# Hybrid decoder layer: the output projection in another token order, the down part's first blocks in other memory, the last norm's left sums made in an earlier product

## The chip, the cores and the metric

The kernel runs on one core of a Trainium2 chip, in one launch. A core has TensorE (PE, matmuls, with a separate queue PEld for weight loads), VectorE (DVE), ScalarE (ACT), GpSimd (POOL) and SyncE (SP), which here issues all large transfers. Engines run their own instruction lists in order and wait for one another by semaphores. The metric is device microseconds (us) of one execution; lower is better.

## The reference

One layer for 1024 tokens of width 1024, all in float32, cut to its last part:

```python
def rmsnorm(x, g):
    y = x * lax.rsqrt(jnp.mean(x * x, axis=-1, keepdims=True) + NORM_EPS) * g
...
h = rmsnorm(x, norm_mix)
# h @ w_in feeds a sparse attention (nsa_out) and a retention (ret_out)
mix = sigmoid(gate_a) * (nsa_out @ w_proj_a) + sigmoid(gate_b) * (ret_out @ w_proj_b)
x = x + mix @ w_out
h = rmsnorm(x, norm_mlp)
x = x + jnp.square(jax.nn.relu(h @ w_up)) @ w_down        # hidden width 4096
return rmsnorm(x, norm_final)
```

The change touches everything from `mix @ w_out` on.

## The kernel before, in words

**Number format.** A float32 operand is split into a high and a low part (`h`, `l`; `bh`, `bl`; `wh`, `wl`): ACT copies it to the high part, DVE (or POOL) subtracts that from the original. A product is then three matmuls, high x high, high x low and low x high, added up in a PSUM bank; one is 128x128 by 128x512.

**Output projection** (lines 1144 to 1170). For each half `c` of the output columns and each of the eight token tiles `j` (128 tokens), `dense_tok` makes `mix @ w_out` on PE, and DVE adds the residual (`x1t`, line 1157). In the second half `norm_a` (ACT: sum of squares) and POOL (`rstd`) make the norm, and DVE the normed tile `h` (line 198; named h2 in the code). The normed tile is then transposed by PE into two banks (`put_t`, `tp<-ident,h`, line 1102; there are two such banks) by one of two functions:

- `first_half`, tiles 0 to 3: the transposes are split into `bh` and `bl`.
- `second_half`, tiles 4 to 7: they are combined with the transposes of tile `j-4` into four more forms of the up part's moving operand (sums and differences of the token halves and of the input halves). The tile `j-4` is rebuilt by POOL as `bh + bl` (lines 1122, 1123). The forms go to `bh`/`bl` and to `th`/`tl` (line 1107).

`later` and `tick` put this work `T_LAG` = 4 ticks behind: a tick comes after every second k-block of a product, so the transposes of a tile stand on PE behind the dense product of the tile that comes two later. Those of the last two tiles stand among the first products of the up part (`up_first(0)`, `up_first(1)`).

**Up part.** `h @ w_up` in 16 pairs `p` of hidden blocks. Each pair takes seven products instead of eight (a scheme of sums and differences): forms 11, 21, 2, 3, 1, 4 and 22 of the tokens against as many forms of the weights (`sf` is a sum or difference of weight blocks, lines 1182 to 1185; `wh`, `wl` are split by line 1025/1026). Forms 2, 3 and 4 are read from `th`/`tl`. The results `u11`, `u21`, `u12`, `u22` and the sums `s1`, `s2`, `s4` go to `u_scr` in device memory (line 1221).

**Down part.** Seven products again, `n` = 1, 2, 7, 6, 5, 4, 3, each of 8 groups of 24 matmuls: hidden values from `u_scr` (line 1253, `raw`) against blocks of `w_down` (line 1259; `y11` are the eight blocks of the first product). They are added up in `ac1` to `ac4` on ACT, DVE and POOL; `add_x1` adds the residual on POOL.

**Finish.** `finish` makes the last norm of a token tile: ACT squares and sums both column halves, POOL adds the two sums and makes `rstd` (lines 1302, 188, 189), DVE scales both halves (line 1306), SP stores. Tiles 4 to 7 are finished in the last product, tiles 0 to 3 at the very end: there PE makes the last twelve matmuls of a tile, DVE adds the bank to `ac1` (line 1352), then comes `finish`.

**What sets the order.** Each engine's instructions keep the order that a scheduler gave them at build time from the program text; memory areas (pools) can be reused, and then the first writer of the new area waits for the last reader of the old one. The pool `res` (eight tiles of 128x1024) lies on the right side over areas of the up part.

## Time and profile before

| | us |
|---|---|
| median of 3 runs | 1624.87 |
| lowest, highest | 1623.61, 1625.33 |
| the profiled execution | 1623.7 |
| its span | 1621.9 |
| PE busy in it | 1566.8 |

The span runs from the first to the last instruction of the profiled execution; its own time is 1.8 us more than that. The granted clock of TensorE was 0.986 of full speed on average. The out projection's second half runs from about 916 to 967, the up part from there to 1296, the down part to 1611.

### The profile page before, as it was taken

What the parts mean: (1) busy time and instruction counts of PE and PEld (TensorE: products, weight loads), DVE (VectorE), ACT (ScalarE), POOL (GpSimd) and SP (SyncE); (2) the same over time, 40 slices, a digit from 0 to 9 for tenths busy, and PEclk for the clock granted to TensorE, in tenths of its full rate; (3) what the DMA queues carried; (4) which work ended last, traced back from release to release, by engine and by line L of the source; (5) the groups of instructions that cost most, each with busy time, mean ns of one, the idle gap of its engine ahead of it and who ended that gap; (6) DMA issues with size and microseconds to landing.
All of it is one profiled execution on the core that took longest, in us unless ns stands there. A gap on an engine that the chain in (4) does not pass through costs nothing.

```text
span 1621.9 us, 22739 instructions
## 1 busy us (share of the span) xinstructions
PE 1566.8 (97%) x7876; PEld 1306.9 (81%) x7876; DVE 1037.2 (64%) x2127; ACT 727.1 (45%) x1611; POOL 484.8 (30%) x565
## 2 busy tenths in 40 slices
PE   7999999999999999999999996999999989999997
PEld 5888887987888888888788874888888768888885
DVE  5665663564777777776654268766666548776464
ACT  5454454664766766676421144222222134343352
POOL 5110010001323323333000035665555216523561
PEclk8999999999999999999999997999999999999999
DMA  6101110252111111121644431444444497763472
GB/s 218 65 14 66 56 32 25 83 171 75 44 36 53 47 33 59 47 66 53 201 150 149 156 104 65 152 165 158 157 148 143 145 324 266 233 206 120 140 255 102
DMA packets 99347, 193.93 MB, mean 120 GB/s; under 512 B 26016, under 2 KB 28448, under 8 KB 99232
## 3 DMA queue, kind: packets, MB, share of 16 engines
q1 hardware_dynamic: 99232, 192.48, 35.1%
q8 instruction: 62, 1.02, 0.3%
q14 instruction: 53, 0.43, 0.1%
HBM read 142.11 MB, written 50.33 MB: 119 GB/s over the span
## 4 chain that ended last, share of the span: by engine, by line
PE 84%; POOL 4%; DVE 4%; ACT 4%; issue 2%; DMA 2%; SPq 0%; DVEq 0%; POOLq 0%; ACTq 0%
PE mm L154 23%; PE mmu L154 22%; PE mmd L154 16%; PE gps L154 8%; PE S L154 4%; PE O L154 3%; PE pt L890 2%; PE pt L889 2%; ACT pW L844 1%; DVE S L835 1%; PE pO L154 1%; DVE pl L892 1%; PE pc L154 1%; POOL ac L1312 1%; ACT pS L844 1%
## 5 line engine op out<-in xcount | busy, mean ns | idle before, releaser
L1025 ACT ACTIVATE wh<-raw 128x1024 fp32r<-128x1024 f32 x120 | 123.7, 1056 | 292.7 <-PE mmu L154 141.1
L1026 DVE TENSOR_TENSOR wl<-raw,wh 128x1024 fp32r<-128x1024 f32 x120 | 183.6, 1554 | 89.8 <-ACT wh L1025 89.8
L154 PE MATMUL mmd<-wh 128*128 128x512 f32 x448 | 175.5, 392 | 6.1 <-ACT wh L1025 6.1
L154 PE MATMUL mm<-wh,bh 128*128 128x512 f32 (+1 forms) x448 | 177.0, 395 | 1.5 <-ACT n L578 1.0
L154 PE MATMUL mmd<-wl,wh 128*128 128x512 f32 x448 | 175.4, 392 | 1.0 <-DVE wl L1026 1.0
L154 PE MATMUL mmd<-wh,wl 128*128 128x512 f32 x448 | 175.2, 391 | 0.0
L154 PE MATMUL mm<-wh,bl 128*128 128x512 f32 (+1 forms) x448 | 171.3, 382 | 2.7 <-DVE bl L208 2.7
L154 PE MATMUL mm<-wl,bh 128*128 128x512 f32 (+1 forms) x448 | 171.2, 382 | 0.5 <-DVE wl L182 0.5
L892 DVE TENSOR_TENSOR pl<-pt,ph 128x512 fp32r<-128x512 f32 (+1 forms) x160 | 103.7, 648 | 30.2 <-ACT ph L891 27.7
L188 POOL TENSOR_SCALAR msq<-ssq 128x1 f32<-128x1 f32 (+1 forms) x32 | 7.7, 242 | 372.7 <-ACT h L194 193.0
L891 ACT ACTIVATE ph<-pt 128x512 fp32r<-128x512 f32 (+1 forms) x160 | 90.3, 567 | 55.0 <-PE pt L890 50.4
L854 POOL TENSOR_SCALAR pS<-pS,cf 128x1024 f32<-128x1024 f32 (+7 forms) x64 | 47.8, 748 | 220.3 <-DVE cf L852 69.5
L835 DVE CUSTOM_DVE_ANT_0 S<-S,edge_m 128x512 f32<-128x512 f32 (+3 forms) x192 | 100.6, 530 | 14.9 <-PE S L154 12.9
L154 PE MATMUL gps<-bh,wh 128*128 128x512 f32 x256 | 108.1, 422 | 0.3 <-ACT gst L748 0.2
L154 PEld LDWEIGHTS mmd<-wh 128*128 128x128 f32 x448 | 84.6, 189 | 24.2 <-ACT wh L1025 6.5
L154 PE MATMUL mmu<-bh,wl 128*128 128x512 f32 x256 | 100.4, 392 | 1.5 <-DVE wl L1026 1.5
L154 PEld LDWEIGHTS mm<-wh,bl 128*128 128x128 f32 x448 | 84.7, 189 | 21.2 <-DVE bl L208 3.7
L154 PE MATMUL gps<-bh,wl 128*128 128x512 f32 x256 | 100.9, 394 | 0.0
L154 PE MATMUL gps<-bl,wh 128*128 128x512 f32 x256 | 100.8, 394 | 0.0
L154 PE MATMUL mmu<-bh,wh 128*128 128x512 f32 x256 | 100.6, 393 | 0.0
L154 PE MATMUL mmu<-bl,wh 128*128 128x512 f32 x256 | 100.4, 392 | 0.0
L154 PEld LDWEIGHTS mmd<-wl,wh 128*128 128x128 f32 x448 | 84.7, 189 | 19.5 <-DVE wl L1026 2.0
(294 smaller groups left out, 4051.3 us busy)
## 6 DMA issues: line engine op xcount, KB each, us to landing
raw<-u_scr SPq DMA_DIRECT2D x56, 512.0 KB, 3.9
raw<-w_down SPq DMA_DIRECT2D x40, 512.0 KB, 4.9
raw<-w_up SPq DMA_DIRECT2D x32, 512.0 KB, 3.3
u_scr<-u SPq DMA_DIRECT2D x64, 256.0 KB, 2.0
u_scr<-s SPq DMA_DIRECT2D x48, 256.0 KB, 2.0
y<-w_down SPq DMA_DIRECT2D x16, 512.0 KB, 6.6
x<-x SPq DMA_DIRECT2D x8, 512.0 KB, 3.7
qt<-q_scr SPq DMA_DIRECT2D x32, 128.0 KB, 2.4
```

Source lines behind the costliest of these rows:

```text
L154: T.matmul(o, w, m, start=start, stop=stop)
L188: G.tensor_scalar(m[:, :w], ssq, 1.0 / n, EPS, op0=OP.mult, op1=OP.add)
L835: V.tensor_tensor_reduce(sc, sc, mk, -0.125, BIGPOS, OP.add, OP.min, mx[:, b:b + 1])
L844: A.activation(o, sc, AF.Exp, bias=mx[:, m:m + 1], scale=-1.0, accum_out=sums[:, b:b + 1])
L854: G.tensor_scalar(v, v, cf[:, b:b + 1], 1.0, op0=OP.mult, op1=OP.mult)
L889: T.transpose(tp[:, bi * 2], p0, ident)
L890: T.transpose(tp[:, bi * 2 + 1], p1, ident)
L891: A.activation(ph[:, :n], tp[:, :n], AF.Copy)
L892: V.tensor_sub(pl[:, :n], tp[:, :n], ph[:, :n])
L1025: A.activation(h[:, :n], r, AF.Copy)
L1026: V.tensor_sub(l[:, :n], r, h[:, :n])
L1312: G.tensor_tensor(t, t, x, op=OP.add)
```

## The change

Four things are edited.

1. Tokens go through the out projection in the order 0, 1, 4, 2, 5, 3, 6, 7. `first_half` keeps a plain copy of each bank of transposes (`raw_t`, ACT), and `second_half` uses it in place of the POOL sums `bh + bl`.
2. `th` and `tl` become three pairs of tiles, `t2`, `t3`, `t4`, in the same pool.
3. The eight `y11` blocks get a pool of their own, `res2`, after `acc`; the four banks of the first down product are taken in another order; the first two loads of hidden values are written into the last pair of the up part (`s_load`).
4. `finish`: mean and epsilon are folded into small DVE operations; for tiles 0 to 3 the left half's sum of squares and its multiplication by the norm's gain are made when the product n = 2 is complete and its residual is added (`sums_of`, written in the branch n = 5, placed by the scheduler in the product n = 7), and ACT scales the left half at the end.

The diff, cut to its core:

```diff
@@ -1039,18 +1039,21 @@
-        th_ = formp.tile([P, 12, 512], F32R, name="th")
-        tl_ = formp.tile([P, 12, 512], F32R, name="tl")
+        tf_ = {i: [formp.tile([P, 4, 512], F32R, name=f"t{i}{x}") for x in "hl"] for i in (2, 3, 4)}
...
@@ -1106,32 +1109,33 @@
+            raw_t = {}
+
             def first_half(h, j, q):
                 tp = put_t(h, q)
                 ks = slice(4 * q, 4 * q + 4)
                 split_ps(tp, bh[:, ks, cols(j)], bl[:, ks, cols(j)])
+                raw_t[j, q] = frm.tile([P, 4, P], F32, name=f"raw_t{q}", bufs=2)
+                A.activation(raw_t[j, q], tp, AF.Copy)
 
             def second_half(h, j):
                 i = cols(j - 4)
                 js = cols(j)
+                y11, y21 = raw_t[j - 4, 0], raw_t[j - 4, 1]
...
-                G.tensor_tensor(y11, bh[:, :4, i], bl[:, :4, i], op=OP.add)
-                G.tensor_tensor(y21, bh[:, 4:, i], bl[:, 4:, i], op=OP.add)
                 A.activation(y12, tp, AF.Copy)
-                V.tensor_sub(y11, y12, y11)
+                V.tensor_sub(y11, tp, y11)
...
@@ -1145,14 +1149,14 @@
-                for j in range(NT):
+                for n, j in enumerate((0, 1, 4, 2, 5, 3, 6, 7)):
...
@@ -1220,6 +1224,11 @@
+        def s_load(i, g):
+            r = wraw.tile([P, 1024], F32, name="raw", tag="raw")
+            nc.sync.dma_start(r, flat(u_scr[i][:, 2 * g:2 * g + 2]))
+            return r
@@ -1228,6 +1237,8 @@
+            else:
+                s_raw0 = [s_load(0, 0), s_load(0, 1)]
             up_rest(p, X, s, p < 2)
@@ -1237,21 +1248,17 @@
     res = ctx.enter_context(tc.tile_pool(name="res", bufs=8, side="right", reuse_waits="tile"))
+    acc = ctx.enter_context(tc.tile_pool(name="acc", bufs=4, side="right", reuse_waits="tile"))
+    res2 = ctx.enter_context(tc.tile_pool(name="res2", bufs=8, side="right", reuse_waits="tile"))
     wr7 = ctx.enter_context(tc.tile_pool(name="wr7", bufs=3, reuse_waits="tile"))
     rw2 = ctx.enter_context(tc.tile_pool(name="rw2", bufs=3, reuse_waits="tile"))
-    acc = ctx.enter_context(tc.tile_pool(name="acc", bufs=4, side="right", reuse_waits="tile"))
...
-            t = y11[g] = wd(0, 0, g, res, name="y11")
+            t = y11[g] = wd(0, 0, g, res2, name="y11")
@@ -1293,17 +1300,28 @@
+    def sums_of(t, o):
+        y = tmp.tile([P, 512], F32, name="yq8")
+        A.activation(y, t, AF.Square, accum_out=o)
+
-    def finish(j, c0, c1):
+    def finish(j, c0, c1, pre=None):
         ss = tmp.tile([P, 2], F32, name="ss8")
         y = tmp.tile([P, D], F32, name="y8")
-        for c, t in ((0, c0), (1, c1)):
-            A.activation(y[:, c * 512:(c + 1) * 512], t, AF.Square, accum_out=ss[:, c:c + 1])
-        sq = tmp.tile([P, 1], F32, name="sq8")
-        G.tensor_add(sq, ss[:, 0:1], ss[:, 1:2])
-        r = rstd_of(sq, D, tmp)
+        if pre is None:
+            sums_of(c0, ss[:, 0:1])
+            pre = tmp.tile([P, 1], F32, name="pre8")
+            V.tensor_scalar(pre, ss[:, 0:1], 1.0 / D, EPS, op0=OP.mult, op1=OP.add)
+        sums_of(c1, ss[:, 1:2])
+        m = tmp.tile([P, 1], F32, name="m8")
+        r = tmp.tile([P, 1], F32, name="r8")
+        V.scalar_tensor_tensor(m, ss[:, 1:2], 1.0 / D, pre, op0=OP.mult, op1=OP.add)
+        G.tensor_tensor(r, m, nhalf[:, :1], op=OP.pow)
         for c, t in ((0, c0), (1, c1)):
             cs = slice(c * 512, (c + 1) * 512)
-            V.scalar_tensor_tensor(y[:, cs], t, r, gain3[:, cs], op0=OP.mult, op1=OP.mult)
+            if c == 0 and j < 4:
+                A.activation(y[:, cs], t, AF.Copy, scale=r)
+            else:
+                V.scalar_tensor_tensor(y[:, cs], t, r, gain3[:, cs], op0=OP.mult, op1=OP.mult)
...
+        if step == 0:
+            bank = bank[2:] + bank[:2]
...
             elif n == 5:
                 A.activation(A4[i], b, AF.Copy)
                 G.tensor_tensor(A1[i], A1[i], A4[i], op=OP.add)
+                sums_of(A2[i], pres[i][:, 1:2])
+                V.tensor_scalar(pres[i][:, 0:1], pres[i][:, 1:2], 1.0 / D, EPS, op0=OP.mult, op1=OP.add)
+                G.tensor_tensor(A2[i], A2[i], gain3[:, :512], op=OP.mult)
...
-                finish(i, A2[i], A1[i])
+                finish(i, A2[i], A1[i], pres[i][:, 0:1])
```

How instructions move, at three places. First DVE at the end of the out projection, before: `x1t` of tile 7 is added, `wl` is the low part of the first up weights, and then comes the second half of tile 6 (`y11_10856` and on).

```order
L1107 TENSOR_TENSOR tl_10176<-y21_10789,th_10175 128x4x128
L1157 TENSOR_TENSOR x1t_10823<-mmu_10826,x1t_10823 128x512
L1026 TENSOR_TENSOR wl_10902<-raw_10899,wh_10901 128x1024
L1125 TENSOR_TENSOR y11_10856<-y12_10857,y11_10856 128x512
L198 SCALAR_TENSOR_TENSOR h2_10885<-x1t_10823,rstd_10889,gain_10189 128x1024
L1127 TENSOR_TENSOR f2_10859<-tp_10864,y11_10856 128x512
L1128 TENSOR_TENSOR y12_10857<-tp_10864,y12_10857 128x512
```

The same place of the changed kernel: `bl_84<-tp_10876` and `bl_84<-tp_10916` are the low parts of tile 3, and tile 6's second half begins with `raw_t0_10762`, the kept copy of tile 2.

```order
L1110 TENSOR_TENSOR t4l_10180<-raw_t1_10670,t4h_10179 128x4x128
L1161 TENSOR_TENSOR x1t_10848<-mmu_10851,x1t_10848 128x512
L1110 TENSOR_TENSOR bl_84<-tp_10876,bh_83 128x4x128
L1026 TENSOR_TENSOR wl_10905<-raw_10902,wh_10904 128x1024
L198 SCALAR_TENSOR_TENSOR h2_10888<-x1t_10848,rstd_10892,gain_10193 128x1024
L1110 TENSOR_TENSOR bl_84<-tp_10916,bh_83 128x4x128
L1129 TENSOR_TENSOR raw_t0_10762<-tp_10948,raw_t0_10762 128x512
```

Tile 3's first half has moved behind the last dense product's addition, where before tile 5's second half had just ended; the second halves of tiles 6 and 7 follow in both.

The second place is SP's list at the end of the up part, before: stores of the last pair (`u11_13270` to `s4_13338`), a load of hidden values (`raw_13541`) and the first blocks of `w_down` (`y11_...`).

```order
L1221 DMA u_scr0_76<-u11_13270 128x512
L1221 DMA u_scr5_81<-u22_13300 128x512
L1221 DMA u_scr1_77<-u21_13301 128x512
L1253 DMA raw_13541<-u_scr0_76 128x1024
L1259 DMA y11_13403<-w_down 128x2x512
L1221 DMA u_scr2_78<-u12_13302 128x512
L1221 DMA u_scr3_79<-s2_13337 128x512
L1221 DMA u_scr4_80<-s1_13336 128x512
L1221 DMA u_scr6_82<-s4_13338 128x512
L1259 DMA y11_13439<-w_down 128x2x512
L1259 DMA y11_13475<-w_down 128x2x512
```

The same list of the changed kernel:

```order
L1225 DMA u_scr0_76<-u11_13278 128x512
L1225 DMA u_scr5_81<-u22_13308 128x512
L1266 DMA y11_13416<-w_down 128x2x512
L1225 DMA u_scr1_77<-u21_13309 128x512
L1266 DMA y11_13450<-w_down 128x2x512
L1266 DMA y11_13486<-w_down 128x2x512
L1225 DMA u_scr2_78<-u12_13310 128x512
L1225 DMA u_scr3_79<-s2_13345 128x512
L1225 DMA u_scr4_80<-s1_13344 128x512
L1225 DMA u_scr6_82<-s4_13346 128x512
L1266 DMA y11_13522<-w_down 128x2x512
L1229 DMA raw_13552<-u_scr0_76 128x1024
```

The first `w_down` block stands two places earlier, the next two stand ahead of the stores of `u12` and of the sums, and the load of hidden values stands behind them.

The third place is DVE's end of the program, two of the last four tiles, before:

```order
L1352 TENSOR_TENSOR ac1_13377<-mmd_15317,ac1_13377 128x512
L1306 SCALAR_TENSOR_TENSOR y8_15575<-ac2_13381,rstd_15581,gain_13375 128x512
L1306 SCALAR_TENSOR_TENSOR y8_15575<-ac1_13377,rstd_15581,gain_13375 128x512
L1352 TENSOR_TENSOR ac1_13378<-mmd_15318,ac1_13378 128x512
L1306 SCALAR_TENSOR_TENSOR y8_15602<-ac2_13382,rstd_15608,gain_13375 128x512
L1306 SCALAR_TENSOR_TENSOR y8_15602<-ac1_13378,rstd_15608,gain_13375 128x512
```

and of the changed kernel, where `m8` is 128x1:

```order
L1376 TENSOR_TENSOR ac1_13392<-mmd_15352,ac1_13392 128x512
L1317 SCALAR_TENSOR_TENSOR m8_15613<-ss8_15609,pre_13388 128x1
L1324 SCALAR_TENSOR_TENSOR y8_15610<-ac1_13392,r8_15614,gain_13386 128x512
L1376 TENSOR_TENSOR ac1_13393<-mmd_15353,ac1_13393 128x512
L1317 SCALAR_TENSOR_TENSOR m8_15638<-ss8_15634,pre_13389 128x1
L1324 SCALAR_TENSOR_TENSOR y8_15635<-ac1_13393,r8_15639,gain_13386 128x512
```

One of the two 128x512 scalings has gone to ACT, and a 128x1 operation has come.

## Rows read from the trace of the kernel before

In a row of the timeline the columns are: start in us, length in us, engine, line, operation, output<-inputs, shapes, number of instructions, and in brackets the idle time ahead of it with what ended it.

**Rows 1.** The page: PE's busy time with share and instructions (first row), and PE's busy tenths in 40 equal slices of the span (second row).

```profile
PE 1566.8 (97%) x7876; PEld 1306.9 (81%) x7876; DVE 1037.2 (64%) x2127; ACT 727.1 (45%) x1611; POOL 484.8 (30%) x565
...
PE   7999999999999999999999996999999989999997
```

**Rows 2.** Windows of the span. Columns: window, its length, busy us (and instructions) of PE, PEld, DVE, ACT, POOL, then the granted clock of TensorE, the DMA engines' busy share, GB/s.

```profile
970.00:990.00 20.00, 9.80 (x38) 7.21 (x37) 18.17 (x18) 9.20 (x16) 15.64 (x12) 0.76 0.04 14
990.00:1010.00 20.00, 13.87 (x52) 10.57 (x51) 15.68 (x20) 8.14 (x12) 10.74 (x8) 0.82 0.26 85
...
1290.00:1310.00 20.00, 12.96 (x47) 9.94 (x46) 9.15 (x11) 4.85 (x5) 5.01 (x4) 0.83 0.61 209
...
1610.00:1622.00 12.00, 0.94 (x5) 0.44 (x3) 4.91 (x8) 2.17 (x6) 1.86 (x6) 0.71 0.34 131
```

**Rows 3.** PE's waits from 860 us to the end. Columns: what waits, what for, us in total, times, longest us.

```profile
PE tp L1102 <- DVE bl L1107: 7.5, 2, 4.6
PE mmd L154 <- ACT wh L1025: 6.1, 1, 6.1
```

**Rows 4.** Timeline of PE around the first seam: transposes of tile 5, second matmul of the first up product, second transposes of tile 7, and the first matmul behind the last stop.

```profile
966.56 1.03 PE L1102 MATMUL tp<-ident,h 128*128 128x128 f32 x8
...
967.66 0.40 PE L154 MATMUL mmu<-bl,wh 128*128 128x512 f32 x1
...
985.92 1.09 PE L1102 MATMUL tp<-ident,h 128*128 128x128 f32 x4 [2.93 <-DVE bl L1107]
...
1001.27 0.80 PE L154 MATMUL mmu<-th,wl 128*128 128x512 f32 x1 [4.36 <-DVE wl L1026]
```

**Rows 5.** Timeline of DVE from the last dense products to the first seam: residual additions of three tiles, the first subtraction of a second half, and `sf`.

```profile
947.59 0.69 DVE L1157 TENSOR_TENSOR x1t<-mmu,x1t 128x512 f32<-128x512 f32 x1
...
953.99 0.69 DVE L1157 TENSOR_TENSOR x1t<-mmu,x1t 128x512 f32<-128x512 f32 x1
...
961.45 0.69 DVE L1125 TENSOR_TENSOR y<-y,y 128x512 f32<-128x512 f32 x1 [0.38 <-ACT y L1124]
...
969.65 0.68 DVE L1157 TENSOR_TENSOR x1t<-mmu,x1t 128x512 f32<-128x512 f32 x1
...
991.43 1.78 DVE L1184 TENSOR_TENSOR sf<-raw 128x512 f32<-128x512 f32 x1 [1.18 <-POOL raw L1183]
```

**Rows 6.** Timelines of ACT (a high part from a bank) and of POOL at the first seam.

```profile
941.63 0.60 ACT L1106 ACTIVATE bh<-tp 128x512 fp32r<-128x512 f32 x1 [2.88 <-PE tp L1102]
...
984.59 1.72 POOL L1130 TENSOR_TENSOR y<-y,f 128x512 f32<-128x512 f32 x1
986.27 1.75 POOL L1122 TENSOR_TENSOR y<-bh,bl 128x512 f32<-128x512 f32 x1
...
991.36 1.30 POOL L1123 TENSOR_TENSOR y<-bh,bl 128x512 f32<-128x512 f32 x1
```

**Rows 7.** The second seam: timelines of PE, ACT, DVE and of SP's queue, the DMA issues between 1280 and 1300 us (out<-in, queue, count, KB each, median us from issue to landing), and a window (columns as in rows 2).

```profile
1302.30 0.80 PE L154 MATMUL mmd<-wh 128*128 128x512 f32 x1 [6.09 <-ACT wh L1025]
1304.05 0.80 PE L154 MATMUL mmd<-wl,wh 128*128 128x512 f32 x1 [0.95 <-DVE wl L1026]
...
1301.19 1.06 ACT L1025 ACTIVATE wh<-y 128x1024 fp32r<-128x1024 f32 x1 [6.83 <-DMA y<-w_down]
...
1302.28 1.72 DVE L1026 TENSOR_TENSOR wl<-y,wh 128x1024 fp32r<-128x1024 f32 x1 [4.61 <-ACT wh L1025]
...
1292.78 2.57 SPq L1221 DMA_DIRECT2D u_scr<-u  x2
...
1296.58 0.39 SPq L1259 DMA_DIRECT2D y<-w_down  x1
...
raw<-u_scr SPq DMA_DIRECT2D x1, 512.0 KB, 3.6
y<-w_down SPq DMA_DIRECT2D x1, 512.0 KB, 4.5
...
1304.00:1308.00 4.00, 3.95 (x9) 3.18 (x10) 0.00 (x0) 0.73 (x1) 0.00 (x0) 0.51 0.96 317
```

**Rows 8.** The tail: DVE and POOL for the last two tiles in the timeline, and DVE's group of an operation on 128x1 (busy us, mean ns of one).

```profile
1610.80 0.68 DVE L1352 TENSOR_TENSOR ac<-mmd,ac 128x512 f32<-128x512 f32 x1
...
1614.79 0.68 DVE L1352 TENSOR_TENSOR ac<-mmd,ac 128x512 f32<-128x512 f32 x1
...
1616.30 0.19 POOL L1302 TENSOR_TENSOR sq<-ss 128x1 f32<-128x1 f32 x1 [2.88 <-ACT y L1300]
...
1616.86 0.55 POOL L189 TENSOR_TENSOR rstd<-msq,nhalf 128x1 f32<-128x1 f32 x1
1617.44 1.41 DVE L1306 SCALAR_TENSOR_TENSOR y<-ac,rstd,gain 128x512 f32<-128x512 f32 x2 [1.97 <-POOL rstd L189]
...
L840 DVE TENSOR_TENSOR mx<-mx 128x1 f32<-128x1 f32 x64 | 10.4, 162 | 0.2
```

**Rows 9.** Timelines of ACT (splits of a group) and of POOL (residual additions) in the third product of the down part.

```profile
1392.78 2.01 ACT L1025 ACTIVATE wh<-raw 128x1024 fp32r<-128x1024 f32 x2 [3.43 <-PE mmd L154]
1398.22 2.01 ACT L1025 ACTIVATE wh<-raw 128x1024 fp32r<-128x1024 f32 x2 [3.43 <-PE mmd L154]
...
1393.02 5.77 POOL L1312 TENSOR_TENSOR ac<-ac,x 128x512 f32<-128x512 f32 x3
...
1401.10 2.27 POOL L1312 TENSOR_TENSOR ac<-ac,x 128x512 f32<-128x512 f32 x1
```

More of the change, by code (lines that the diff above doesn't have):

```diff
@@ L1051, in y_form @@
         def y_form(i, k):
[L1052 to L1053 removed]
+            if i in tf_:
+                return tf_[i][0][:, k], tf_[i][1][:, k]
+            H, L, k0, ts = {11: (bh, bl, 0, t1), 21: (bh, bl, 4, t1), 22: (bh, bl, 4, t2), 1: (bh, bl, 0, t2)}[i]
             return H[:, k0 + k, ts], L[:, k0 + k, ts]
@@ L1116, in second_half @@
                 js = cols(j)
+                y11, y21 = raw_t[j - 4, 0], raw_t[j - 4, 1]
+                y12 = frm.tile([P, 4, P], F32, name="y12")
+                f2 = frm.tile([P, 4, P], F32, name="f2")
                 tp = put_t(h, 0)
[L1118 to L1123 removed]
                 A.activation(y12, tp, AF.Copy)
[L1125 removed]
+                V.tensor_sub(y11, tp, y11)
                 tp = put_t(h, 1)
@@ L1154, in hybrid_block @@
                     dense_tok(ps, j, W)
-                    if c == 0 and j == NT - 1:
+                    if c == 0 and n == NT - 1:
                         W = out_w(1)
@@ L1246, in hybrid_block @@
     y11, y12 = {}, {}
-    def flat(t):
-        return t.rearrange("p a b -> p (a b)")
     def s_group(i, g):
-        r = wraw.tile([P, 1024], F32, name="raw", tag="raw")
-        nc.sync.dma_start(r, flat(u_scr[i][:, 2 * g:2 * g + 2]))
-        return split_t1024(r)
+        return split_t1024(s_raw0[g] if i == 0 and g < 2 else s_load(i, g))
     def wd(b, c, g, pool, **kw):
@@ L1312, in add_x1 @@
         G.tensor_tensor(t, t, x, op=OP.add)
+    pres = [acc.tile([P, 2], F32, name="pre") for _ in range(4)]
     A1, A2, A3, A4 = new_acc("ac1"), new_acc("ac2"), new_acc("ac3"), new_acc("ac4")
```

14 lines of the change are left out of this document (5 added, 9 removed).

## The prediction

> **What bounds the kernel now.** The page's first two parts come first [rows 1]: TensorE (PE) is busy for 97% of the span, and its slices are full but for the first, two in the middle and the last. An edit off PE is worth only what it takes out of such holes. The windows put numbers to those that this change can reach [rows 2]: PE is busy for 9.80 of 20 us in 970–990, 13.87 of 20 in 990–1010 (out projection to up part, the first seam), 12.96 of 20 in 1290–1310 (up to down part, the second) and 0.94 of 12 after 1610 (the tail). In the first three the granted clock is 0.76 to 0.83 as well: each stop is followed by a stretch at the lower of the two levels (1.2 instead of 2.4 GHz). The waits of PE name VectorE's (DVE's) low parts and a late weight split [rows 3]. So I price each seam by itself and take everything else as covered.
>
> The sum is made against the profiled execution, 1623.7 us, 1.2 below the median of the runs, 1624.87; I carry the difference over to that median.
>
> **Part 1: interleaved tokens and kept transposes (first seam).** Removed are eight POOL additions that rebuild a transposed half from its high and low parts; eight ScalarE (ACT) copies out of PSUM are added. The order changes so that one second half stands between first halves, and only those of tiles 6 and 7 are left when the dense products end; before, four stood in a row. What ends the seam before: PE's last transposes, of tile 7, start at 985.92, and products run without a stop only from 1001.27 on [rows 4], when the low part of `sf` is ready, which stands behind tile 7's list on DVE. The granted clock is below full there [rows 2], after the stops.
>
> Step one, where PE gets to. A second half holds DVE for 8.2 us (from its first subtraction at 961.45 to the next token's addition at 969.65), while a token's period is 6.4 (947.59 to 953.99) [rows 5]. With single second halves DVE falls 1.8 behind and recovers in the next slots. The kept copy adds about 0.6 us to the time that a transposes' bank is held (a copy of that shape takes 0.60 [rows 6]). I get one new stop of PE of 1.1 to 1.4 us and one of 0.3: the dense products end at about 968.2 instead of 966.5 [rows 4].
>
> Here the third read of a bank must be priced. In the trace, ACT's high part starts at 941.63 and takes 0.60, and DVE's low part of the same bank comes after it, so I queue the copy as a third turn; ACT stood idle for 2.88 us ahead of that row, waiting for PE, and that idle time is the cover [rows 6]. If the cover were gone for all eight copies, they would cost 8 x 0.60 = 4.8 us. The Trainium skill (PSUM — Partial Sum Buffer, "PSUM bank collisions raise a hardware error") says that two engines may not touch one bank in the same partitions at once, reads included, and that a compiler puts a dependency between them. By that rule the copies can never run beside DVE's read; the trace agrees, as the two reads follow each other. The rule speaks against this edit, and the sum by it alone would be the 4.8 us worse.
>
> Step two, the last two tiles. DVE's addition for tile 7 starts at about 970.2 (969.65 before [rows 5]), and the low part of tile 3's last half, which now stands ahead of it, lets the second matmul of the first up product start at about 971.5 (967.66 before [rows 4]). Twenty-three matmuls 0.227 us apart (24 make the 5.44 us between the ACT rows 1392.78 and 1398.22 [rows 9]) and four transposes at 0.1 make 5.6: 977.1. Two ACT copies (0.60 in the row, a little less from start to start) make 978.25; then DVE's subtraction 0.7, ACT's high part 0.6, POOL's low part 1.5 and the `y21` subtraction 1.5, the middle of POOL's 1.30 to 1.75 at this size [rows 6]: tile 6 is done at about 982.6, and not at 986.31 (984.59 + 1.72). From there to 1001.27 it took 14.9 us. In that list POOL's addition of 1.75 (at 986.27) is gone, and the one of 1.30 (at 991.36), which ran beside DVE's `sf` of 1.78 where an operation of that size takes 0.68 (969.65), is gone too, so `sf` loses 1.1 [rows 5, 6]. That leaves 12.1: PE resumes at 994.7. Gain 6.5 us. Low end 4.5 (POOL at the long ends of its rows, 0.4 twice, and another 1.2 for one more stop of the kind in step one); high end 8.5 (with shorter stops the clock stays up and 2 us come back, about what nine matmuls lose at the lower clock in [rows 7]).
>
> **Part 2: the down part's first transfers (second seam).** PE stands for 6.09 us until 1302.30, for ACT's high part of the first `w_down` block (`y`, 1301.19 + 1.06), then until 1304.05 for DVE's low part (1302.28 + 1.72). The block was issued at 1296.58 and took 4.5 us to land. It sat behind the stores and a 512 KB load on SP, and its memory waited for the last up product. In the changed order it stands straight behind the `u22` store (in the group at 1292.78), and its memory is the area of form 2 to 4's high and low parts, done by then. I put the issue at 1293.2; 4.1 us to land (between 3.6, the `raw` of the same size, and 4.5) gives 1297.3, ACT 1.06 more 1298.4, DVE 1.72 more 1300.2: the second matmul comes 3.85 earlier [rows 7]. The four loads of hidden values that the diff writes ahead of time (`s_raw0`) stand on SP at the same place as before; I cost them at nothing. The other blocks of `w_down` come later or earlier by one or two places; each has a group of 24 matmuls, 5.44 us, as cover, and without it one would cost about its 4 us of flight. The clock: from 1304.00 nine matmuls are busy for 3.95 us at a granted 0.51, the lower level, 1.9 more than at 0.227 each. With a stop shorter by 4 us some of that goes; between 0 and 1.9 I take 1.0. Gain 4.8; ends 3.2 (landing 4.5, no clock) and 6.4 (landing 3.6, all of it).
>
> **Part 3: sums made apart (the tail).** The last four tiles run in series on DVE: additions at 1610.80 and 1614.79, a period of 3.99 us, while PE's twelve matmuls for a tile need 2.72. In it: from the addition to POOL's start 1.51 (1616.30), two small POOL operations 0.56 (1616.86 less 1616.30), then 0.58 to DVE's scaling of 1.41 for two halves (1617.44) [rows 8]. After: 1.51, one DVE operation on 128x1 in place of the two on POOL, not in the trace in this form: between the 0.16 of the 128x1 `mx` row and the 0.28 that each POOL operation took with its gap, I take 0.2; 0.58; one scaling of 0.70, with ACT scaling the other half beside it. The sum is 2.99, with hand-overs 3.07. Three periods give 2.8, the last chain 0.65 (its second store is issued by the later of two engines). Gain 3.4; ends 2.6 (ACT's scaling is the later one and the next square queues behind it, 0.2 to 0.3 a tile) and 4.3 (0.3 less a tile).
>
> What is taken out of the tail is paid earlier: ACT's four sums of the left half, four POOL multiplications and four small DVE operations. They run in the third product. ACT's sums wait for POOL's additions of residuals (1393.02 for 5.77, then one at 1401.10 to 1403.4), so the split that ran at 1398.22 comes at 1405.7 to 1407.8, and its low part by about 1410 [rows 9]. Splits run three to four groups of 5.44 us ahead (1392.78 to 1398.22 is one group in that chain), so PE wants this one at about 1414.5: 4.5 us to spare, price 0. If that cover went, each us past it would be a us of PE.
>
> **Sum.** 6.5 + 4.8 + 3.4 = 14.7: 1609.0 for a profiled execution, 1610.2 for the median.
>
> **Rivals.**
> (a) The first seam gives only about 4, because the new order makes longer stops than the 1.7 us of step one, or the kept copies don't find ACT idle. For it: PE's waits there already are for DVE's low parts [rows 3], and a bank is held longer. Against: ACT's 2.88 us of idle time. Four instead of 6.5 gives 1612.7; with all 4.8 of the copies on the path, 1615.0.
> (b) The early `w_down` transfer gains nothing: it lands late among the stores (2 x 256 KB ahead of it), or the split stands behind another wait on ACT. For it: the DMA engines are 0.96 busy a little later, in 1304–1308 [rows 7]. Against: ACT has been idle for 6.83 us ahead of that split and waits for the transfer alone. A gain of 1.2 in place of 4.8 gives 1613.8.
> (c) More: clock restored in both seams, POOL's rows at their short end: the high ends 8.5, 6.4, 4.3 are 19.2, or 1605.7; I put this case at about 1605.
> (d) Slower than before: ACT blocks in the third product. Its sums stand in its queue ahead of the splits; if POOL's additions came late, every split behind them would, and PE would stop. To undo the gain and be slower by 0.2% the delay would have to pass the 4.5 us to spare by 14.7 + 3.2 = 18 us. POOL's four additions end by 1403.4 and the multiplications stand behind them, so I see no such source.
>
> **How the numbers follow.** Forecast 0.70 (itself 1606.5 to 1613), (a) 0.11, (b) 0.08, (c) 0.06, (d) or no change at all 0.05. The prediction is 1610.2. The range 1604.5 to 1616.0 reaches from (c) past (a) with all its copies; it leaves out (d) and the far ends. About 0.2%, or 3.2 us, is what a measurement of this kernel can tell from no change; forecast, (a), (b) and (c) are all faster by more: 0.95, with 0.02 for the same and 0.03 for slower.
>
> **What would show it.** In the changed profile: PE's restart after the second pair of late transposes at about 994–996 and no POOL additions there; two short stops of PE before the dense products end; the first `y<-w_down` issued near 1293 less the 6.5 gained, and PE's second matmul of the down part some 3.8 us sooner after the last of the up part; last additions 3.0 to 3.1 us apart; no wait of PE on a split around the end of the third product's first half. The prediction is wrong if PE's waits for DVE's low parts between the last dense product and the up part stay near their sum of today, or if new waits of PE stand in the down part.

## The result, and the profile after

The changed kernel takes 1614.52 us (median of 6 runs, 1612.03 to 1616.63), the kernel before 1625.1 (median of the 6 runs beside it, 1623.61 to 1627.99). The ratio is 0.993, with a 95% interval of 0.9916 to 0.9943: faster by about 10.6 us. Predicted were 1610.2, a gain of 14.7 to 14.9, with a range of 1604.5 to 1616.0. The direction and the places were right; the gain is some 4 us smaller than the sum: 1614.52 is inside the range, but outside the forecast's own 1606.5 to 1613 and among the times of rival (a), 1612.7 to 1615.0. Two runs below had executions of 3162.92 to 5597.37 us among ones near 1615 to 1625 (one of four, two of ten), which are left out of their medians.

The page of the changed kernel, its profiled execution with a span of 1610.2 us (its own time 1612.03), against [rows 1]:

```profile
PE 1567.9 (97%) x7876; PEld 1306.5 (81%) x7876; DVE 1039.1 (65%) x2139; ACT 734.3 (46%) x1623; POOL 483.0 (30%) x545
...
PE   8999999999999999999999997999999999999998
```

The windows at the seams (columns as in [rows 2]; the second seam and the tail have moved forward by about 9 and 11 us):

```profile
970.00:990.00 20.00, 15.26 (x67) 11.99 (x68) 14.50 (x19) 11.38 (x20) 9.42 (x8) 0.91 0.05 15
990.00:1010.00 20.00, 15.64 (x61) 12.30 (x60) 16.49 (x21) 5.69 (x8) 7.60 (x7) 0.91 0.45 143
...
1280.00:1300.00 20.00, 16.71 (x61) 12.95 (x60) 13.88 (x15) 6.02 (x6) 7.49 (x4) 0.83 0.46 154
...
1600.00:1611.00 11.00, 2.46 (x11) 1.69 (x10) 3.52 (x7) 3.36 (x7) 1.10 (x2) 0.84 0.37 143
```

PE is busy for 30.9 of 40 us in the first seam, where it was 23.7. The clock in the second seam is 0.83 in both kernels: PE stands for less there, and still pays for it.

To say how much each stretch gave, I take the starts of PE's matmuls with the same number in both traces (5000, before the first seam; 5300, behind it; 6700, behind the second) and the end of the span; of kernels with added matmuls these are skipped in the count. The lengths of the four stretches, in us, with the difference to the kernel before in brackets:

| profiled execution | up to 5000 | first seam | second seam | rest with tail | median of runs |
|---|---|---|---|---|---|
| before | 933.69 | 83.11 | 327.05 | 278.07 | 1625.1 |
| after | 932.06 (-1.63) | 79.34 (-3.77) | 323.89 (-3.15) | 274.95 (-3.12) | 1614.52 |
| predicted | 0 | -6.5 | -4.8 | -3.4 | -14.7 |

The first column ends ahead of the first seam. I take those -1.63 us as this execution's chance (in the runs below the column lies between -1.89 and +2.39); the three seams then give 10.0 us, which agrees with the 10.6 of the medians.

PE's waits from 860 us on, against [rows 3] (what waits, what for, us in total, times, longest):

```profile
PE mmu L154 <- DVE wl L1026: 4.4, 1, 4.4
PE tp L1105 <- DVE bl L1110: 2.6, 1, 2.6
PE mmd L154 <- ACT wh L1025: 2.4, 1, 2.4
PE tp L1105 <- ACT raw_t L1119: 2.3, 2, 2.1
```

The wait for the first `w_down` block's split fell from 6.1 to 2.4, the transposes' for DVE from 7.5 to 2.6, and a new one is there: for the kept copy `raw_t`. Its place in PE's timeline, and what comes after it up to the first product of form 2 (against [rows 4]):

```profile
961.62 0.66 PE L1105 MATMUL tp<-ident,h 128*128 128x128 f32 x4 [2.09 <-ACT raw_t L1119]
...
964.10 0.63 PE L154 MATMUL mmu<-wh,bl 128*128 128x512 f32 x1
...
971.46 0.50 PE L154 MATMUL mmu<-bl,wh 128*128 128x512 f32 x1 [0.52 <-DVE bl L1110]
...
983.00 1.08 PE L1105 MATMUL tp<-ident,h 128*128 128x128 f32 x4 [2.60 <-DVE bl L1110]
...
995.58 0.50 PE L154 MATMUL mmu<-t2h,wl 128*128 128x512 f32 x1 [4.36 <-DVE wl L1026]
```

A matmul that takes 0.63 here, and starts 0.43 behind the one before it, runs at the lower level; at the full one it is 0.39 and 0.23. The granted clock in the two windows behind the new stop:

```profile
961.60:964.00 2.40, 2.38 (x9) 2.00 (x10) 1.81 (x3) 2.12 (x4) 0.37 (x2) 0.64 0.84 306
964.00:966.00 2.00, 2.00 (x7) 1.53 (x7) 1.76 (x2) 1.23 (x2) 2.00 (x3) 0.58 0.01 5
```

ACT's copy that PE waits for, with DVE's norm of another tile and the low part ahead of it; DVE's addition for tile 7 with the low part behind it; and the end of tile 6 on POOL, against [rows 5, 6]:

```profile
959.05 1.28 DVE L198 SCALAR_TENSOR_TENSOR h<-x1t,rstd,gain 128x1024 f32<-128x1024 f32 x1 [2.67 <-POOL rstd L189]
960.25 0.68 DVE L1110 TENSOR_TENSOR bl<-tp,bh 128x512 fp32r<-128x512 f32 x1
960.97 0.60 ACT L1119 ACTIVATE raw_t<-tp 128x512 f32<-128x512 f32 x1 [2.37 <-DVE bl L1110]
...
970.13 0.68 DVE L1161 TENSOR_TENSOR x1t<-mmu,x1t 128x512 f32<-128x512 f32 x1
970.73 0.68 DVE L1110 TENSOR_TENSOR bl<-tp,bh 128x512 fp32r<-128x512 f32 x1
...
981.66 1.73 POOL L1135 TENSOR_TENSOR raw_t<-raw_t,f 128x512 f32<-128x512 f32 x1
```

The second seam, against [rows 7]: the block's issue behind the `u22` store, its split, PE's first two matmuls, and a window of what follows.

```profile
1287.39 0.32 SPq L1225 DMA_DIRECT2D u_scr<-u  x1
1287.80 0.39 SPq L1266 DMA_DIRECT2D y<-w_down  x1
...
1292.06 1.06 ACT L1025 ACTIVATE wh<-y 128x1024 fp32r<-128x1024 f32 x1 [3.09 <-DMA y<-w_down]
...
1293.17 0.65 PE L154 MATMUL mmd<-wh 128*128 128x512 f32 x1 [2.35 <-ACT wh L1025]
1294.76 0.79 PE L154 MATMUL mmd<-wl,wh 128*128 128x512 f32 x1 [0.94 <-DVE wl L1026]
...
1295.00:1298.00 3.00, 3.00 (x8) 2.32 (x9) 2.48 (x2) 3.00 (x4) 3.00 (x2) 0.50 0.25 92
```

The tail, against [rows 8]: additions for three of the last four tiles, the 128x1 operation of one of them, and POOL's only operation.

```profile
1597.38 0.68 DVE L1376 TENSOR_TENSOR ac<-mmd,ac 128x512 f32<-128x512 f32 x1
...
1598.85 0.16 DVE L1317 SCALAR_TENSOR_TENSOR m<-ss,pre 128x1 f32<-128x1 f32 x1 [0.79 <-ACT yq L1305]
1599.16 0.55 POOL L1318 TENSOR_TENSOR r<-m,nhalf 128x1 f32<-128x1 f32 x1 [2.48 <-DVE m L1317]
...
1600.41 0.69 DVE L1376 TENSOR_TENSOR ac<-mmd,ac 128x512 f32<-128x512 f32 x1
...
1603.44 0.69 DVE L1376 TENSOR_TENSOR ac<-mmd,ac 128x512 f32<-128x512 f32 x1
```

### The profile page after: what moved, and what is told of

Its sections match the earlier page's. It is cut to its first block, busy times and chain, and to the rows that moved or that the text cites. A ratio compares the mean times of both kernels' runs of the same rounds, so it can differ in the third digit from the quotient of the medians.

```text
span 1610.2 us, 22745 instructions
## 1 busy us (share of the span) xinstructions
PE 1567.9 (97%) x7876; PEld 1306.5 (81%) x7876; DVE 1039.1 (65%) x2139; ACT 734.3 (46%) x1623; POOL 483.0 (30%) x545
## 4 chain that ended last, share of the span: by engine, by line
PE 83%; DVE 4%; POOL 4%; ACT 3%; issue 2%; DMA 2%; SPq 0%; POOLq 0%; ACTq 0%; DVEq 0%
PE mm L154 23%; PE mmu L154 22%; PE mmd L154 16%; PE gps L154 8%; PE S L154 4%; PE O L154 3%; PE pt L890 2%; PE pt L889 2%; ACT pW L844 1%; DVE S L835 1%; PE pO L154 1%; DVE pl L892 1%; PE pc L154 1%; POOL ac L1330 1%; ACT pS L844 1%
## 5 line engine op out<-in xcount | busy, mean ns | idle before, releaser
L1026 DVE TENSOR_TENSOR wl<-raw,wh 128x1024 fp32r<-128x1024 f32 x120 | 189.2, 1603 | 74.3 <-ACT wh L1025 74.0
L835 DVE CUSTOM_DVE_ANT_0 S<-S,edge_m 128x512 f32<-128x512 f32 (+3 forms) x192 | 100.7, 530 | 14.9 <-PE S L154 12.9
```

The lines of the kernel that those rows point to most:

```text
L835: V.tensor_tensor_reduce(sc, sc, mk, -0.125, BIGPOS, OP.add, OP.min, mx[:, b:b + 1])
L1026: V.tensor_sub(l[:, :n], r, h[:, :n])
```

## The experiments

The questions were whether the parts stand by themselves, what the new stop for `raw_t` costs, and whether PE's stops or something else bring the lower clock. For each run the table at the end of this section has the stretches.

**The order alone.** Edit to the kernel before:

```diff
-                for j in range(NT):
+                for n, j in enumerate((0, 1, 4, 2, 5, 3, 6, 7)):
...
-                    if c == 0 and j == NT - 1:
+                    if c == 0 and n == NT - 1:
```

Expected: 

> The kernel before with the token order 0, 1, 4, 2, 5, 3, 6, 7 and nothing else: no kept copies, POOL still rebuilds the first halves by two additions a tile. Theory A (the kept copy holds the bank as a third turn, and that makes the new 2.09 us stop of PE before the dense products end, and with it 1.5 us of lower clock): the stop is under 0.9 us here and the clock stays at the full level in front of the up part; the POOL additions are back in the last two tiles' chain (1.8 to 2.9 us), so the seam gains about 2 to 4 us: 1621 to 1623. Rival B (the order itself, with a second half that holds DVE for some 8 us, makes the stop; the copies don't matter for it): the stop stays at 1.5 to 3 us with the lower clock behind it, and the seam gains 0 to 2 us: 1623 to 1626.

Measured: 1626.31 us, ratio to before 1.0006 (0.9997 to 1.0016). Neither theory had it: the first seam loses 2.4 us. The stop that theory A is about is shorter (1.08 us, now for DVE's low part), but PE then stands for 4.54 us in front of the second matmul of the up part:

```profile
962.13 0.63 PE L1102 MATMUL tp<-ident,h 128*128 128x128 f32 x4 [1.08 <-DVE bl L1107]
...
974.40 0.80 PE L154 MATMUL mmu<-bl,wh 128*128 128x512 f32 x1 [4.54 <-DVE bl L1107]
...
971.74 2.00 DVE L1026 TENSOR_TENSOR wl<-raw,wh 128x1024 fp32r<-128x1024 f32 x1
973.66 0.68 DVE L1107 TENSOR_TENSOR bl<-tp,bh 128x512 fp32r<-128x512 f32 x1
```

In this build DVE makes `wl` of the first up weights, 2.00 us, ahead of the low part of tile 3 that PE waits for; in the changed kernel it stands behind it. So I put 2 us of the loss down to the scheduler's order, by that length; no run turns it alone. In this build the order by itself gains nothing.

**The first part undone.** The changed kernel with the token order and the two functions of before (`range(NT)`, `G.tensor_tensor(y11, bh..., bl..., op=OP.add)` and so on).

Expected: 

> The changed kernel with token order and POOL additions of the kernel before: only the second seam and the tail are changed. If the three parts stand by themselves, it takes what the aligned traces give for seam two and tail: 3.2 + 3.2 = 6.4 us less than before, 1618.7 us, and the rest of the change, 3.9 us, is the first seam's. If the first seam is worth nothing (its gain in the trace would then be an offset that the profiled execution had by chance), the time is that of the changed kernel, 1614.5.

Measured: 1618.48 us, ratio 0.9956 (0.9942 to 0.9971). The parts add up: 4.0 us of the change's gain are the first seam's, 3.77 in the trace. But this execution's second seam gained 5.69, not 3.15. PE's stops there are as long as the changed kernel's, and the matmuls behind them are at full clock:

```profile
1298.15 0.49 PE L154 MATMUL mmd<-wh 128*128 128x512 f32 x1 [1.94 <-ACT wh L1025]
1300.15 0.50 PE L154 MATMUL mmd<-wl,wh 128*128 128x512 f32 x1 [1.51 <-DVE wl L1026]
...
1300.00:1304.00 4.00, 3.85 (x17) 3.18 (x18) 3.30 (x3) 3.61 (x4) 3.92 (x3) 1.00 0.20 74
```

So 2.5 us of the second seam are the clock's, and they come or don't behind stops of about one length. This execution is the fastest of the run's four by 3 us (1614.88; the others 1617.88 to 1620.39), so the median may stand for executions in which the clock fell.

**The second part alone.** The kernel before with `t2` to `t4`, `res2`, the bank order and `s_load`, and nothing else.

Expected: 

> The kernel before with the second part alone (t2 to t4 as tiles of their own, y11 in res2, the bank order, the two loads written ahead). Additive reading: first seam 4.0 (changed kernel against the run with the first part undone), tail 3.1 (three periods from 3.99 to 3.03 and the shorter last chain), so the second seam gives what is left of 10.6, 3.5 us: 1621.6 to 1622. If the tail gave nothing in the median, this run takes what the run with second and third part takes, 1618.5.

Measured: 1622.01 us, ratio 0.9986 (0.9976 to 0.9996), as expected: the medians say 2.5 to 3.1, and the 3.5 us are inside the interval, 0.7 to 3.9. The trace has -3.43 in the second seam and +0.02 in the tail, and it has the lower clock, behind stops that are hardly different from those of the run above:

```profile
1298.80 0.68 PE L154 MATMUL mmd<-wh 128*128 128x512 f32 x1 [1.85 <-ACT wh L1025]
1300.89 0.79 PE L154 MATMUL mmd<-wl,wh 128*128 128x512 f32 x1 [1.41 <-DVE wl L1026]
...
1301.00:1305.00 4.00, 4.00 (x10) 3.13 (x11) 3.48 (x2) 3.33 (x4) 3.92 (x3) 0.50 0.19 72
```

**A filler at the second seam, holding a weight slot.** Thirteen matmuls of no use behind the last up product of the changed kernel:

```diff
+        spare = psW.tile([P, 512], F32, name="spare", tag="mm")
+        for k in range(13):
+            mm(spare, X[4][0][:, :P], y_form(22, k % 4)[0], True, True)
     bigs.close()
```

Expected: 

> The changed kernel with 13 matmuls of no use (128x128 by 128x512, 2.95 us at full clock, into a bank that nobody reads) behind the last product of the up part, where PE stands for 2.35 us. Theory C (the stop itself brings the lower clock, which costs 2.6 us there): PE doesn't stand before the first matmul of the down part, the clock stays up or falls for less, and the time drops by 1.5 to 2.6 us, to 1612 to 1613. Rival D (the clock falls for another reason, such as what the DMA engines and the other engines do then): the clock falls as before, and the time is the changed kernel's or up to 0.6 us above it, 1614.5 to 1615.1.

Measured: 1614.59 us, ratio 0.9937 (0.9917 to 0.9956): no gain, and not a test of the clock. The filler reads the last weights' slot, and the first block's split writes that slot:

```profile
1295.94 2.00 ACT L1025 ACTIVATE wh<-y 128x1024 fp32r<-128x1024 f32 x2 [4.83 <-PE spare L154]
```

The split came later than it could, PE stood again for 1.15 and 0.77 us behind the filler, and the clock fell.

**A filler that holds nothing.** Fifteen matmuls of a constant zero tile instead; `fill` below is used in the later runs too.

```diff
+        idle = idlep.tile([P, 512], mybir.dt.bfloat16, name="idle")
+        V.memset(idle, 0.0)
+
+        def fill(pool, n, tag):
+            ps = pool.tile([P, 512], F32, name="spare", tag=tag)
+            for _ in range(n):
+                mm(ps, idle[:, :P], idle, True, True)
...
+        fill(psW, 15, "mm")
     bigs.close()
```

Expected: 

> The changed kernel with 15 matmuls of no use behind the up part's last product, now of a constant zero tile (bf16, 128x128 by 128x512), so that they hold no weight slot that the next split waits for; in the earlier filler run ACT's split of the first w_down block stood for the filler's slot. Theory C (the stop of PE brings the lower clock, 2.6 us of it): the split is no later than in the changed kernel, PE is without a stop of over 1 us, the lower clock goes for the most part, and the aligned traces show 1.5 to 2.6 us gained behind the seam: about 1612 to 1613. Rival D (the clock falls there anyway): the matmuls after the seam still take 0.43 us each for some 5 us, gain 0 to 0.5 us: 1614 to 1614.5.

Measured: 1610.89 us, ratio 0.991 (0.9893 to 0.9926); 3.6 us below the changed kernel, and -5.70 in the second seam. Nothing of use is earlier here than in the changed kernel; only PE is kept busy, and the clock stays up:

```profile
1293.44 3.41 PE L154 MATMUL spare<-idle 128*128 128x512 bf16 x15
...
1297.55 0.50 PE L154 MATMUL mmd<-wl,wh 128*128 128x512 f32 x1 [0.47 <-DVE wl L1026]
1297.89 0.40 PE L154 MATMUL mmd<-wh,wl 128*128 128x512 f32 x1
```

With PE kept busy the clock stayed up, here and in the two later runs with this filler (-5.70, -5.71 and -5.73), so rival D falls. The other way round it isn't so simple: the run with the first part undone kept its clock with the stops in place. The trace's second seam shows 2.55 us over the changed kernel, the medians 3.6; the difference is less than what executions of one kernel spread by (1612.03 to 1616.63 for the changed one).

**One read of all first halves.** ACT makes the kept copy first, and both parts are split from the copy:

```diff
-                split_ps(tp, bh[:, ks, cols(j)], bl[:, ks, cols(j)])
                 raw_t[j, q] = frm.tile([P, 4, P], F32, name=f"raw_t{q}", bufs=2)
                 A.activation(raw_t[j, q], tp, AF.Copy)
+                split_ps(raw_t[j, q], bh[:, ks, cols(j)], bl[:, ks, cols(j)])
```

Expected: 

> The changed kernel with the first halves read from PSUM once: ACT makes the kept copy first, and high and low part are then split from the copy, so a bank is held for one turn, not three. Theory A: the stop of 2.09 us before the dense products end shrinks to under 0.9 us, the clock stays up there, and the time drops by 2 to 3 us: 1611.5 to 1612.5. Rival B: the stop stays, as DVE's list makes it, and the time stays within 1 us of 1614.5; DVE's low part from SBUF beside POOL may even cost 1 us.

Measured: 1615.19 us, ratio 0.9936 (0.9921 to 0.9951): no gain. The stop is gone (the eight transposes stand in one piece), as theory A says, and PE stands 1.54 and 2.90 us in front of the up part instead, because the scheduler has put `wl` ahead of tile 3's low part, as in the run with the order alone:

```profile
962.55 1.03 PE L1105 MATMUL tp<-ident,h 128*128 128x128 f32 x8
...
974.46 0.80 PE L154 MATMUL mmu<-bl,wh 128*128 128x512 f32 x1 [2.90 <-DVE bl L1110]
```

**One read of tiles 0 to 2 only**, with which DVE's list is the changed kernel's:

```diff
+                if j < 3:
+                    A.activation(raw_t[j, q], tp, AF.Copy)
+                    split_ps(raw_t[j, q], bh[:, ks, cols(j)], bl[:, ks, cols(j)])
+                else:
+                    split_ps(tp, bh[:, ks, cols(j)], bl[:, ks, cols(j)])
+                    A.activation(raw_t[j, q], tp, AF.Copy)
```

Expected: 

> The changed kernel with the first halves of tiles 0, 1 and 2 read from PSUM once (copy first, split from the copy) and tile 3 as in the changed kernel, so that DVE's list is the changed kernel's word for word; in the run with all four tiles, DVE's low part of the first up weights had moved ahead of tile 3's low part. Theory A2 (the bank held by the kept copy sets the 2.09 us stop, and DVE's list behind it is what follows): the stop is gone, DVE's addition for tile 7 comes about 2 us earlier than in the changed kernel (relative to the dense products' start), PE's wait moves to tile 3's low part in front of the up part (about 3 us in all, with the lower clock behind it), and PE's restart after the seam comes 1 to 2 us earlier: 1612.5 to 1613.5. Rival E (the seam is bound by DVE's list, which does not begin earlier): nothing gained at the restart, 1614.5.

Measured: 1612.45 us, ratio 0.9918 (0.9903 to 0.9933), which is 2.1 below the changed kernel, as A2 expected. Its profiled execution doesn't show that gain where A2 put it: the first seam has -3.49 there, no better than the changed kernel's -3.77, and the second -5.69, the outcome without the lower clock, on which this edit has no hold. What A2 says of the bank is there: the stop for `raw_t` is gone and tile 3's low part ends 2.2 us earlier (971.4 in a trace whose stretch up to 5000 is 2.2 longer than the changed kernel's). But PE now waits 2.60 us for it in one piece, and seventeen matmuls from there on, four of them transposes, are at the lower clock:

```profile
971.45 0.79 PE L154 MATMUL mmu<-bl,wh 128*128 128x512 f32 x1 [2.60 <-DVE bl L1110]
...
971.00:977.60 6.60, 6.15 (x17) 4.89 (x18) 2.19 (x3) 2.43 (x5) 0.74 (x2) 0.50 0.11 40
```

What the bank gave, the clock took. Whether the 2.1 us of the medians are the bank's in other executions, or the second seam's clock, this run doesn't settle; the one with both edits, below, shows what the bank is worth where the clock stays up.

**Fillers in the first seam too** (4 and 11 zero matmuls ahead of tile 7's transposes, 20 ahead of the first product of form 2, 15 at the second seam).

Expected: 

> The changed kernel with matmuls of no use in three holes: 4 and 11 in front of tile 7's two groups of transposes, 20 in front of the up part's first product of form 2, and 15 at the second seam. Theory C: the lower clock after the holes of the first seam (6 matmuls and 8 matmuls at 0.43 us, 1.2 and 1.6 us lost) goes too, so the aligned traces show 2 to 2.8 us gained in the first seam over the run that fills the second alone: about 1609.5 to 1611.5. Rival D: no gain in the first seam; where a filler is longer than the hole, up to 0.5 us lost.

Measured: 1610.00 us, ratio 0.9903 (0.9887 to 0.9918). The trace has -5.35 in the first seam, 2.06 better than the run with the second seam filled alone, the low end of theory C's 2 to 2.8; the median is 0.9 below that run's, and inside the forecast. Against the changed kernel the seam is 1.6 better, and all of it lies behind the last stop: PE's restart comes no earlier (995.37 in a trace 1.89 ahead, for 995.58 in one 1.63 ahead), but the matmuls behind it start 0.23 apart, not 0.43. The stop for `raw_t` (2.12 us here) and the wait in front of the up part (2.08 us) were not filled, and in this execution the clock is 1.00 behind both.

**One read of tiles 0 to 2, and all holes filled** (13 more in front of the first up product).

Expected: 

> Tiles 0 to 2 read once, and all holes filled, with 13 more matmuls of no use in front of the first up product, where the wait for tile 3's low part is expected. If both theories (A2 and C) hold, their gains add up and this is the fastest: 1607 to 1610. If the bank does not bind (rival E) or the clock falls anyway (rival D), it is not below 1612.

Measured: 1607.44 us, ratio 0.9889 (0.9874 to 0.9903), with -7.53 in the first seam and the clock at 1.00 in it. With the filler, PE takes up the products as soon as tile 3's low part is there, and at full clock:

```profile
966.09 2.97 PE L154 MATMUL spare<-idle 128*128 128x512 bf16 x13
970.07 0.50 PE L154 MATMUL mmu<-bl,wh 128*128 128x512 f32 x1 [0.78 <-DVE bl L1119]
...
970.00:976.00 6.00, 5.93 (x28) 4.87 (x29) 3.03 (x4) 2.74 (x6) 0.74 (x2) 1.00 0.12 44
```

Between this run and the one before it stand only the one read and the filler of 13: 2.2 us in the trace and 2.6 in the median. The run with fillers alone had the clock at 1.00 there too, so the filler of 13 gave nothing back in this pair of traces; the second up matmul is 2.2 us earlier (970.07 in a trace 0.88 ahead, for 971.25 in one 1.89 ahead), as in the run with the one read alone. So reading the banks of tiles 0 to 2 once is worth about 2 us, and they show only where the clock doesn't take them back.

**The first block early.** The changed kernel, with the first `w_down` block loaded during the last but one pair into a tile of its own and split, with the first hidden values, into weight slots that are free by then:

```diff
+            if p == 14:
+                y0 = wd(0, 0, 0, y0p, name="y0")
             up_rest(p, X, s, p < 2)
+            if p == 15:
+                s_split[0] = split_t1024(s_raw0[0])
+                t_split[0] = split_t1024(y0)
...
-    use_ring(wring, wring, wr5, wr5, wr5, wr7, wr7, wr7)
+    use_ring(wr5, wring, wring, wr7, wr7, wr7, wr5, wr5)
```

Expected: 

> The changed kernel in which the first w_down block is loaded during the last but one pair of the up part into a tile of its own and split, with the first hidden values, into weight slots that are free by then (its other copy, for a later product, is loaded as before). Theory F (at the second seam PE waits for that block's way: issue behind the u22 store, landing, split; nothing else is late): PE goes from the up part into the down part with a stop under 1 us and the clock stays up; later groups may be late by 1 to 2 us. Gain 4 to 6 us on the changed kernel: 1608.5 to 1610.5. Rival G (the next thing is late at once: group 1's split or DVE's low part, so the stop only moves by one group): gain 0 to 2 us, 1612.5 to 1614.5.

Measured: 1609.43 us, ratio 0.9914 (0.9899 to 0.9929), 5.1 below the changed kernel; -8.50 in the second seam. PE goes through without a stop, and the only one left in the first three groups is 0.92 us in the second:

```profile
1290.00:1294.00 4.00, 4.00 (x20) 3.30 (x19) 1.89 (x3) 0.00 (x0) 0.00 (x0) 1.00 0.29 110
1294.00:1298.00 4.00, 4.00 (x19) 3.34 (x18) 2.68 (x4) 0.00 (x0) 0.00 (x0) 1.00 0.97 295
...
1303.21 0.50 PE L154 MATMUL mmd<-wl,wh 128*128 128x512 f32 x1 [0.92 <-DVE wl L1033]
```

Theory F holds: nothing but that block's way was late. Its first seam has only -1.47 in this execution: the clock stayed up behind the 2.11 us stop for `raw_t`, PE then waited 2.1 us for tile 3's low part instead of 0.5, and the clock fell there.

**All of it**: one read of tiles 0 to 2, the first seam's fillers, the block early.

Expected: 

> One read of tiles 0 to 2, the first seam's holes filled with matmuls of no use, and the first w_down block early, with no filler at the second seam. If F holds, it is 2 to 4 us faster than the run with one read and all holes filled (1607.4): 1603.5 to 1605.5. If rival G holds, it is at 1606 to 1610, with the second seam's stop and lower clock back one group later.

Measured: 1606.15 us (1604.71 to 1607.12), ratio 0.9888 (0.9871 to 0.9904): the fastest, 8.4 us below the changed kernel. It is 0.6 above F's range and at the lower edge of G's, but the trace speaks for F: the second seam has -8.49 with no stop in front of it. What is missing is in no seam: the three together are 2.57 us shorter than in the run with one read and fillers, as F had it, while the stretch up to 5000, where the edits put nothing on PE, is 1.88 longer than before (0.88 shorter in that run). Whether that is chance is open; the run with the block early has the same +1.89.

The stretches of the profiled executions, as differences to the kernel before (us), and the medians:

| run | up to 5000 | first seam | second seam | rest with tail | median |
|---|---|---|---|---|---|
| after | -1.63 | -3.77 | -3.15 | -3.12 | 1614.52 |
| order alone | +0.29 | +2.38 | +0.21 | +0.03 | 1626.31 |
| second part alone | +0.27 | +0.47 | -3.43 | +0.02 | 1622.01 |
| first part undone | -0.41 | +0.41 | -5.69 | -3.16 | 1618.48 |
| filler holding a slot | +0.25 | -3.51 | -2.72 | -3.13 | 1614.59 |
| filler holding nothing | +0.68 | -3.29 | -5.70 | -3.13 | 1610.89 |
| one read of all | +2.39 | -3.07 | -4.05 | -3.20 | 1615.19 |
| one read of tiles 0 to 2 | +0.52 | -3.49 | -5.69 | -3.15 | 1612.45 |
| fillers in both seams | -1.89 | -5.35 | -5.71 | -3.15 | 1610.00 |
| one read and fillers | -0.88 | -7.53 | -5.73 | -3.17 | 1607.44 |
| first block early | +1.89 | -1.47 | -8.50 | -3.10 | 1609.43 |
| all of it | +1.88 | -7.59 | -8.49 | -2.92 | 1606.15 |

## Why the prediction was right, and where its sizes were off

**First seam: 6.5 forecast, 3.8 measured.** The failed step is step one. It forecast a new stop of 1.1 to 1.4 us and one of 0.3; in the trace they are 2.09 and 0.18. And it let only 0.55 us of them reach DVE's addition for tile 7 (970.2, where it was 969.65); the addition started at 970.13 in a trace that was already 1.63 us ahead, so at 971.76 in the terms of the one before: 2.1 later, the whole stop. Where the stop is gone (one read of tiles 0 to 2) the addition is at 970.12 in a trace 0.52 behind, at 969.6 as before. The second matmul of the first up product, forecast at 971.5, waits for the low part behind that addition (0.69 and 0.52 us of stops on PE) and was late by the same 1.6: 971.46 and 1.63. Step two's chain from there to tile 6 was forecast as 11.1 us and took 11.9 (971.46 to 983.39, the end of POOL's row 981.66), so tile 6 is 2.4 late in all. The last step, 12.1 us from tile 6 to PE's restart, measured 12.2 (983.39 to 995.58), which agrees with the price of POOL's two additions. What was left of the 6.5 is 4.1; from the restart to matmul 5300 it takes 15.82 us for 15.52 before, with more matmuls at the lower clock, and that is the last 0.3. The 3.8 are below the low end of 4.5. Rival (a), "only about 4, because the new order makes longer stops", with a chance of 0.11, was the better description of this seam.

The rule that spoke against the edit, the Trainium skill (PSUM — Partial Sum Buffer, "PSUM bank collisions raise a hardware error"), names the mechanism of the stop: two engines don't read one bank at once. The trace agrees: `raw_t` starts at 960.97, behind DVE's low part of the same bank, for which ACT waited 2.37 us, and PE waits for the bank until that copy is done. The pair that the prediction showed, ACT's high part and then DVE's low part, was no sign of it, since the low part is made from the high one; the copy needs nothing of DVE's and waited all the same. I had priced the copy's 0.60 and taken ACT's idle time as its cover; what counted as well is that the copy queues behind DVE, where the low part stands in the list behind the norm of another tile, for which DVE itself waited 2.67 us on POOL. So the copy's own length is the smaller part of the 2.09 us, and with the order alone, without copies, 1.08 us of stop were there. Holding the bank like that costs about 2 us by the runs with fillers; the 4.8 us for all eight copies, which the prediction kept as an outer case, did not come.

**Second seam: 4.8 forecast, 3.15 measured.** The transfers did what was said. The block's issue comes 2.63 us ahead of the last up matmul (1290.43; 1295.82 in the trace before), as forecast (2.62); ACT's split starts 4.26 behind the issue (forecast 4.1), and the second matmul stands 4.33 us behind the last up matmul, where it was 8.23: 3.9 earlier, forecast 3.85. The mis-sized term is the clock: I added 1.0 because the stop is shorter, and 13 matmuls ran at the lower clock instead of nine, 0.75 lost. The ends of this term didn't allow for that, and they were added up wrongly: its own terms give 3.45 and 6.25, not 3.2 and 6.4. It also counts four loads in `s_raw0`, where the diff has two. Which of part 2's edits the earlier issue needs, no run tells apart. The experiments say why a middle value was wrong: where the stops were left as they are, the seam gained 3.2 to 3.4 in two traces in which the clock fell and 5.7 in two in which it didn't; one trace, of the run with all first halves read once, lies between, at 4.05.

**Tail: 3.4 forecast, 3.12 measured.** The period is 3.03 us (1597.38, 1600.41, 1603.44) for a forecast of 3.07, the 128x1 operation 0.16 for 0.2. From the last addition to the end of the span it is about 6.8 (7.1 before), so the last chain gave some 0.3, not 0.65.

**Third product: price 0, as said.** No wait of PE stands between 1300 us and the end in the changed trace. ACT's last sum and the splits behind it, in time for PE:

```profile
1398.34 0.63 ACT L1305 ACTIVATE yq<-ac 128x512 f32<-128x512 f32 x1 [3.86 <-POOL ac L1330]
...
1398.97 4.84 ACT L1025 ACTIVATE wh<-raw 128x1024 fp32r<-128x1024 f32 x5
```

The splits start at 1398.97; this trace is 8.5 us ahead of the one before there, so that is 1407.5 in its terms, inside the 1405.7 to 1407.8 forecast and the 4.5 us to spare. Rival (d) had no ground, and rival (b) neither.

## What to carry to other kernels

A hole of the bounding engine costs its length and what the clock does after it: where a seam can't be closed, price it with both outcomes, and not with their mean. A bank is free only when the last of its readers is through: a copy put behind another engine's read adds its length to that engine's delay, so copy out first and split from the copy. An edit that moves a wait must be followed one step further, since here the time won at the bank was given back by the stop that came next, until that was filled too.

## What the runs showed of the hardware that I had not expected

Of two executions with stops of 1.94 + 1.51 and 1.85 + 1.41 us at the second seam, the first went on at a granted clock of 1.00 and the second at 0.50, and the stop for `raw_t` was followed by the lower clock in the changed kernel (2.09 us) and by the full one in the run with fillers in both seams (2.12 us; its next transposes stand 6.0 us behind it, not 7.55) and in the run with the block early (2.11 us). The prediction had each stop followed by the lower level; already in the trace before, the matmuls behind a stop of 1.54 us, at 972.32, start 0.23 apart at a granted clock of 1.00. The stop's length alone doesn't decide; what does is open.

Matmuls of a zero tile in bf16, 15 in 3.41 us, kept the granted clock at 1.00 through the second seam, and 5.7 us of gain went with them in every trace that had them, as in two of the five traces in which the stops were left.
